# Residual add and RMSNorm on one core: 64 KiB runs, and x and results moved in four groups of every fourth partition

## The chip, the cores and the metric

One NeuronCore of one Trainium2 chip. The metric is device time in microseconds of one execution. The kernel before takes 3724.9 us; its runs lie within 0.1% of each other.

## The reference

```python
x, residual: float32 [32, 2048, 2048]; gamma: ones [2048]; eps = 1e-6
z = x + residual
rms = sqrt(mean(z ** 2, axis=-1, keepdims=True) + eps)
return (z / rms * gamma).astype(float32)
```

65,536 rows of 8 KiB are read twice (x and residual) and written once: 1610.6 MB. There is nothing to reuse.

## The kernel before: what the change touches

The 16 DMA engines take their work from two queues: SyncE's (SP, q1 in the page: x and the stores, 67.2% of the engines' time in the kernel before) and ScalarE's (ACT, q10: the residual, called r below, 32.8%). The packets of a queue that one engine has still to move are called its ring here; the records show the packets, and a ring is called empty when none of them is left. A packet is one record of the trace: the run of one partition, or the 4-byte semaphore packet of 9 ns, here "completion": the records of the kernel before have 3712 for its 232 transfers, 16 each, and as many landings. DVE is VectorE. Tile i of x in four groups is x 0 to x 3, and its stores are store 0 to store 3.

A tile is 128 partitions times 7 rows; each partition's 7 rows are neighbours in memory, one run of 56 KiB. Two slots `z[0]`, `z[1]` take x and are worked on in place; `r_area` of 11 rows takes the residual of two tiles in turn, overlapping by three rows.

```python
R = 7; STEP = 4
z = [sb(f"z{p}", [P, R, D]) for p in range(2)]
r_area = sb("r_area", [P, R + STEP, D])

def sp_turn(sp, t):                       # SyncE, tile i
    i = t.i
    t.wait(sp, "done", -1)                # tile i-1 is finished
    inc(sp.dma_start(out=rows(o_f, i - 1), in_=z[(i - 1) % 2][:, : sizes[i - 1], :]), "s_out", i - 1)
    # ... (last tile cut)
    t.wait(sp, "s_out", -1)               # its store has landed: the slot is free
    load_x(sp, t, 1)                      # x of tile i+1 into that slot

def act_turn(s, t, chain):                # ScalarE, tile i
    for h, (a, b) in enumerate(parts(i)):
        chain.wait()
        t.wait(s, "add_a" if h == 0 else "add_b")
        if h == 0 and i > 0:
            load_r(s, t, 1)               # residual of tile i+1, after the first add of tile i
        inc(act_part(...), "rms_a" if h == 0 else "rms_b", i)   # squares, then the root
```

DVE adds in two parts, takes the reciprocal and scales; ACT squares row by row.

## Time and profile before

| | before |
|---|---|
| time, us (3 runs) | 3724.93 (3724.73 to 3724.96) |
| DVE busy, ACT busy | 62%, 29% |
| DMA share and rate in the middle | 1.00, 434 GB/s |
| bytes at 16 x 27.2 GB/s, an estimate from the packet times of this trace | 3701 us |

The prediction shows the lines that say what bounds it. One more view is needed to follow the argument: the timeline of one tile, cut to what issues transfers (start, length in us, queue, line, what moves).

```profile
1790.20 0.34 SPq L153 DMA_DIRECT2D out_dram<-z  x1
...
1814.55 0.34 ACTq L141 DMA_DIRECT2D r_area<-in_residual_dram  x1
...
1831.02 0.33 SPq L135 DMA_DIRECT2D z<-in_x_dram  x1
...
1841.03 0.34 SPq L153 DMA_DIRECT2D out_dram<-z  x1
```

Read it as two queues that feed the same 16 engines (67.2 + 32.8 = 100.0% of their time). "The hole" below means the moment just before and after 1831.02: a store's last packet is through, the x load that waits for its landing has not begun, and SyncE's ring is empty. The hole is open, and the engine stands idle, when ScalarE's ring is empty too.

### The profile page before, as it was taken

Reading aid. Unit: us, or ns where it says so; the run is one execution under the profiler, and the core shown is the slowest. Engines: PE = TensorE matmul, PEld = TensorE weight load, DVE = VectorE, ACT = ScalarE, POOL = GpSimd, SP = SyncE. Lnnn points to the kernel's source line nnn. Section 1 sums busy time; section 2 is a strip of 40 time slices with the busy share of each in tenths; the row PEclk is TensorE's granted clock in tenths of the full one; section 3 lists DMA queues with packets and bytes.
Section 4 is the critical chain, followed back from the end, with each engine's and each line's share of the span. In section 5 each row is a group of like instructions: output and inputs, shape, how many; then the busy total and the mean of one; then the engine's idle time right before and its main releaser. Section 6 shows DMA issues by size and latency. Waiting matters only on the chain.

```text
span 3723.7 us, 3798 instructions
## 1 busy us (share of the span) xinstructions
DVE 2302.6 (62%) x816; ACT 1072.4 (29%) x1176; POOL 0.2 (0%) x4
## 2 busy tenths in 40 slices
DVE  5666665566665566665566665566665566665566
ACT  2233322233322233322233322233322233322233
POOL 0000000000000000000000000000000000000000
DMA  9999999999999999999999999999999999999999
GB/s 421 431 434 435 434 434 435 434 435 435 434 434 434 434 434 434 434 434 433 434 434 434 434 434 434 434 434 434 434 434 434 434 434 434 434 434 434 434 432 398
DMA packets 32963, 1610.68 MB, mean 433 GB/s; under 512 B 3712, under 2 KB 3776, under 8 KB 3776
## 3 DMA queue, kind: packets, MB, share of 16 engines
q1 hardware_dynamic: 22592, 1082.17, 67.2%
q10 hardware_dynamic: 10368, 528.49, 32.8%
q14 instruction: 3, 0.02, 0.0%
HBM read 1073.77 MB, written 536.87 MB: 433 GB/s over the span
## 4 chain that ended last, share of the span: by engine, by line
DMA 67%; DVE 22%; issue 9%; ACT 2%; SPq 0%; DVEq 0%; ACTq 0%
DMA out_dram<-z 39%; DMA z<-in_x_dram 27%; DVE z L172 15%; DVE z L177 7%; ACT sq_junk L223 1%; ACT rms L231 0%; DVE rstd L197 0%; SPq L259 0%; DVEq L127 0%; DVE r_area L275 0%; ACTq L211 0%; ACTq L127 0%; SPq L141 0%; DVE tail_rstd L292 0%; SPq L162 0%
## 5 line engine op out<-in xcount | busy, mean ns | idle before, releaser
L172 DVE TENSOR_TENSOR z<-z,r_area 128x8192 f32<-128x8192 f32 (+2 forms) x150 | 1109.5, 7437 | 1252.5 <-DMA z<-in_x_dram 1252.5
L223 ACT ACTIVATE sq_junk<-z 128x2048 f32<-128x2048 f32 x512 | 963.4, 1882 | 2617.1 <-DVE z L172 2605.7
L177 DVE SCALAR_TENSOR_TENSOR z<-z,rstd,gamma_tile 128x2048 f32<-128x2048 f32 x505 | 1153.6, 2344 | 5.2
L197 DVE RECIPROCAL rstd<-rms 128x4 f32<-128x4 f32 (+2 forms) x146 | 25.3, 173 | 130.8 <-ACT rms L231 130.8
L223 ACT ACTIVATION_READ_ACCUMULATOR sq_junk<-z 128x1 f32 x512 | 95.5, 186 | 0.0
L231 ACT ACTIVATE rms<-ssq,eps_tile 128x4 f32<-128x4 f32 (+2 forms) x146 | 43.3, 297 | 13.4
L177 DVE SCALAR_TENSOR_TENSOR z<-z,tail_rstd,gamma_tile 128x2048 f32<-128x2048 f32 x7 | 16.2, 2345 | 0.1
L277 DVE LOAD_MASK_SELECT gamma_tile<-r_area x1 | 0.0, 14 | 16.1 <-DMA r_area<-in_gamma_dram 16.1
L277 DVE STREAM_SHUFFLE gamma_tile<-r_area 128x2048 f32<-128x2048 f32 x1 | 2.3, 2290 | 0.0
L275 DVE MEMSET r_area<- 128x2048 f32 x1 | 1.8, 1765 | 0.4 <-issue 0.4
L223 ACT ACT_TABLE_LOAD x1 | 1.3, 1283 | 0.9 <-SPq L77 0.9
L231 ACT ACT_TABLE_LOAD x1 | 1.3, 1283 | 0.1
L231 ACT ACTIVATE tail_rms<-tail_ssq,eps_tile 128x2 f32<-128x2 f32 (+1 forms) x4 | 1.2, 295 | 0.1
L274 DVE MEMSET eps_tile<- 128x1 f32 x1 | 0.1, 59 | 1.0 <-SPq L77 1.0
L292 DVE RECIPROCAL tail_rstd<-tail_rms 128x2 f32<-128x2 f32 (+1 forms) x4 | 0.6, 158 | 0.0
L349 POOL MEMSET const-bfloat16-1.0<- 128x1 bf16 x1 | 0.1, 101 | 0.0
L349 POOL MEMSET const-uint8-127<- 128x1 uint8 x1 | 0.1, 101 | 0.0
L349 POOL MEMSET const-float32-0.0<- 128x1 f32 x1 | 0.1, 98 | 0.2 <-issue 0.2
L349 POOL MEMSET const-float32-1.0<- 128x1 f32 x1 | 0.1, 98 | 0.0
## 6 DMA issues: line engine op xcount, KB each, us to landing
r_area<-in_residual_dram ACTq DMA_DIRECT2D x72, 7168.0 KB, 35.5
z<-in_x_dram SPq DMA_DIRECT2D x71, 7168.0 KB, 27.5
out_dram<-z SPq DMA_DIRECT2D x71, 7168.0 KB, 40.8
z<-in_x_dram SPq DMA_DIRECT2D x3, 2048.0 KB, 17.9
out_dram<-z SPq DMA_DIRECT2D x3, 2048.0 KB, 15.0
r_area<-in_residual_dram SPq DMA_DIRECT2D x1, 5120.0 KB, 25.0
z<-in_x_dram SPq DMA_DIRECT2D x1, 5120.0 KB, 36.7
out_dram<-z SPq DMA_DIRECT2D x1, 5120.0 KB, 26.5
```

The costliest lines, as they stand in the source:

```text
L172: return v.tensor_add(out=s, in0=s, in1=r_area[:, e + a : e + b, :])
L177: ins = v.scalar_tensor_tensor(out=s, in0=s, scalar=rs[:, c + g - a : c + g - a + 1], in1=gamma_tile[:, :], op0=mult, op1=mult,)
L197: v.reciprocal(out=rstd[p][h][:, :n], in_=rms[p][h][:, :n]).then_inc(dve, U)
L223: s.activation(out=sq_junk[:, :], in_=src[:, g, :], func=Act.Square, accum_out=sq[:, g - a : g - a + 1],)
L231: return s.activation(out=rm, in_=sq[:, : b - a], func=Act.Sqrt, bias=eps_tile[:, :], scale=inv_d)
L274: v.memset(eps_tile[:, :], float(eps))
L275: v.memset(stage, 0.0).then_inc(tail_ev["add"], 1)
L277: v.stream_shuffle(gamma_tile[:, :].rearrange("p (a b) -> p a b", a=16), stage, [0] * 32)
L292: v.reciprocal(out=tail_rstd[:, a:b], in_=tail_rms[:, a:b]).then_inc(dve, U)
L349: nc = _bacc.Bacc("TRN2", target_bir_lowering=False, num_devices=1)
```

## The change

Its intent: runs of 64 KiB, so that fewer packets carry the same bytes. Both kernels hold 25 rows a partition: 2 x 7 + 11 before, 2 x 8 + 9 now. So the residual area has only 9 rows, and the residual of the next tile can go out only after seven rows are added. To keep the queue fed all the same, stores and x loads are cut into four groups of 32 partitions (every fourth), and x of a group goes out when the store of that group has landed.

```diff
-    R = 7
-    STEP = 4
+    R = 8
+    AREA = 9
+    Q = 4
...
     def parts(i):
-        return [(STEP, k), (0, STEP)] if i % 2 else [(0, R - STEP), (R - STEP, R)]
+        return [(4, R), (1, 4), (0, 1)] if i % 2 else [(0, 4), (4, R - 1), (R - 1, R)]
...
+    def group(q):
+        return slice(q, P, Q)
+    def load_x(sp, i, q):
+        sp.dma_start(out=z[i % 2][group(q), : sizes[i], :], in_=rows(x_f, i)[group(q)]).then_inc(
+            ev["x_in"][i % 2], U)
...
-    def sp_turn(sp, t):
-        ... (store whole, wait, load whole)
+    def sp_turn(sp, i):
+        def load(q):
+            sp.wait_ge(s_out[q], i * U)
+            load_x(sp, i + 1, q)
+        Turn(i).wait(sp, "done", -1)
+        for q in range(Q - 1):
+            store(sp, i - 1, q)
+        for q in range(Q - 1):
+            load(q)
+        store(sp, i - 1, Q - 1)
+        load(Q - 1)
...
     def act_turn(s, t, chain):
+        t.wait(s, "add_a")
+        squares(s, chain, z[p], a, m, ssq[p][0], 0)      # three rows
+            t.wait(s, "add_b")
+            load_r(s, t, 1)                              # after two adds, 7 rows
+        squares(s, chain, z[p], m, b, ssq[p][0], m - a)
+        ... (root, second half)
```

Cut: names, semaphores, the first tile's residual in a free part of `z[0]`, and the tail (the last tile of 5 rows arrives whole and leaves in three parts; the store of the tile before it leaves in two halves). The order on SyncE: stores 0, 1, 2, then x 0, x 1, x 2, then store 3, then x 3.

More of the change, by code (lines that the diff above doesn't have):

```diff
@@ L38 @@
     n_rows, D = x_f.shape
-    R = 7
-    STEP = 4
+    R = 8
+    AREA = 9
+    Q = 4
     U = 16
-    lead = [3, 5]
-    n_full = (n_rows // P - sum(lead)) // R
-    sizes = lead + [R] * n_full
+    first, final = 3, 5
+    n_full = (n_rows // P - first - final) // R
+    sizes = [first] + [R] * n_full + [final]
     starts = [0]
@@ L50 @@
     last = n_tiles - 1
-    LO = 3
-    n_iter = (last - LO) // 2
+    LO = 1
+    n_iter = (last - 1 - LO) // 2
     HI = LO + 2 * n_iter
-    assert n_iter >= 1
+    assert n_iter >= 1 and last % 2 == 0 and HI == last - 1
     def rows(t, i):
@@ L59, in rows @@
         return t[starts[i] : starts[i] + P * k, :].rearrange("(p r) m -> p r m", r=k)
-    r_full = r_f[starts[2] :, :].rearrange("(n p r) m -> n p r m", p=P, r=R)
+    r_full = r_f[starts[1] : starts[last], :].rearrange("(n p r) m -> n p r m", p=P, r=R)
     inv_d = 1.0 / float(D)
@@ L79 @@
     z = [sb(f"z{p}", [P, R, D]) for p in range(2)]
-    r_area = sb("r_area", [P, R + STEP, D])
+    r_area = sb("r_area", [P, AREA, D])
     eps_tile = sb("eps_tile", [P, 1])
@@ L89 @@
     gamma_tile = ps("gamma_tile", [P, D])
-    names = ["x_in", "r_in", "s_out", "add_a", "add_b", "rms_a", "rms_b", "done"]
+    names = ["x_in", "r_in", "add_a", "add_b", "add_c", "rms_a", "rms_b", "done"]
     ev = {k: [sem(f"{k}{p}") for p in range(2)] for k in names}
-    x_tail = [sem(f"x_tail{k}") for k in range(4)]
+    s_out = [sem(f"s_out{q}") for q in range(Q)]
+    half = sem("half")
     g_in = sem("g_in")
@@ L99, with res, halves @@
     tail_ev = {k: sem(f"tail_{k}") for k in ("add", "rms", "done")}
-    tail = [(0, 2), (2, 4), (4, 6), (6, 7)]
-    def entry(i):
+    tail = [(0, 2), (2, 4), (4, 5)]
+    def res(i, a, b):
         if i == 0:
-            return R + STEP - sizes[0]
-        return 0 if i % 2 else STEP
+            return z[0][:, 5 + a : 5 + b, :]
+        e = 4 if i == last else 0 if i % 2 else 1
+        return r_area[:, e + a : e + b, :]
     def parts(i):
         if i == 0:
-            return [(0, 2), (2, sizes[0])]
-        k = sizes[i] if i < 2 else R
-        return [(STEP, k), (0, STEP)] if i % 2 else [(0, R - STEP), (R - STEP, R)]
+            return [(0, 1), (1, 2), (2, 3)]
+        return [(4, R), (1, 4), (0, 1)] if i % 2 else [(0, 4), (4, R - 1), (R - 1, R)]
+    def halves(i):
+        (a0, b0), (a1, b1), (a2, b2) = parts(i)
+        return [(a0, b0), (min(a1, a2), max(b1, b2))]
     class Turn:
@@ L119, in __init__, with at, whole_x, load_r @@
             self.i, self.it, self.p = i, it, i % 2
-        def at(self, d):
-            n = ((self.i + d) // 2 + 1) * U
-            return n if self.it is None else self.it * (U // 2) + n
+        def at(self, d, u):
+            n = ((self.i + d) // 2 + 1) * u
+            return n if self.it is None else self.it * (u // 2) + n
         def wait(self, eng, kind, d=0):
-            eng.wait_ge(ev[kind][(self.i + d) % 2], self.at(d))
+            u = Q * U if kind == "x_in" else U
+            eng.wait_ge(ev[kind][(self.i + d) % 2], self.at(d, u))
     def inc(ins, kind, i):
         return ins.then_inc(ev[kind][i % 2], U)
-    def load_x(sp, t, d=0):
+    def group(q):
+        return slice(q, P, Q)
+    def load_x(sp, i, q):
+        sp.dma_start(out=z[i % 2][group(q), : sizes[i], :], in_=rows(x_f, i)[group(q)]).then_inc(
+            ev["x_in"][i % 2], U
+        )
+    def whole_x(sp, i):
+        sp.dma_start(out=z[i % 2][:, : sizes[i], :], in_=rows(x_f, i)).then_inc(
+            ev["x_in"][i % 2], Q * U
+        )
+    def load_r(eng, t, d=0):
         i = t.i + d
-        inc(sp.dma_start(out=z[i % 2][:, : sizes[i], :], in_=rows(x_f, i)), "x_in", i)
-    def load_r(sp, t, d=0):
-        i = t.i + d
-        e = entry(i)
-        inc(
-            sp.dma_start(
-                out=r_area[:, e : e + sizes[i], :],
-                in_=rows(r_f, i) if t.it is None else r_full[t.it + (i - 2)],
+        inc(
+            eng.dma_start(
+                out=res(i, 0, sizes[i]),
+                in_=rows(r_f, i) if t.it is None else r_full[t.it + (i - 1)],
             ),
@@ L147, in load_r, with store, store_rows @@
         )
-    def sp_turn(sp, t):
-        i = t.i
-        t.wait(sp, "done", -1)
-        inc(
-            sp.dma_start(out=rows(o_f, i - 1), in_=z[(i - 1) % 2][:, : sizes[i - 1], :]),
-            "s_out",
-            i - 1,
-        )
-        if i == last:
-            return
-        t.wait(sp, "s_out", -1)
-        if i + 1 == last:
-            for k, (a, b) in enumerate(tail):
-                sp.dma_start(
-                    out=z[last % 2][:, a:b, :], in_=rows(x_f, last)[:, a:b, :]
-                ).then_inc(x_tail[k], U)
-        else:
-            load_x(sp, t, 1)
+    def store(sp, i, q):
+        sp.dma_start(out=rows(o_f, i)[group(q)], in_=z[i % 2][group(q), : sizes[i], :]).then_inc(
+            s_out[q], U
+        )
+    def store_rows(sp, i, a, b):
+        sp.dma_start(out=rows(o_f, i)[:, a:b, :], in_=z[i % 2][:, a:b, :]).then_inc(s_tail, U)
+    def sp_turn(sp, i):
[9 more added lines that the diff above has]
+        load(Q - 1)
     def add(v, i, a, b):
-        e = entry(i)
         s = z[i % 2][:, a:b, :]
-        return v.tensor_add(out=s, in0=s, in1=r_area[:, e + a : e + b, :])
+        return v.tensor_add(out=s, in0=s, in1=res(i, a, b))
     def scale(v, i, a, b, rs, c=0):
@@ L190, in dve_turn @@
         t.wait(v, "r_in")
-        (a0, b0), (a1, b1) = parts(i)
-        inc(add(v, i, a0, b0), "add_a", i)
-        inc(add(v, i, a1, b1), "add_b", i)
-        for h, (a, b) in enumerate(parts(i)):
+        for k, (a, b) in zip(("add_a", "add_b", "add_c"), parts(i)):
+            inc(add(v, i, a, b), k, i)
+        for h, (a, b) in enumerate(halves(i)):
             n = b - a
@@ L199, in dve_turn @@
             ins = scale(v, i, a, b, rstd[p][h])
+            if h == 0 and i == last - 1:
+                ins.then_inc(half, 1)
         inc(ins, "done", i)
@@ L215, in next, with squares @@
             self.n += 1
-    def act_part(s, chain, src, a, b, sq, rm):
+    def squares(s, chain, src, a, b, sq, c):
         for g in range(a, b):
-            if g > a:
-                chain.wait()
+            chain.wait()
             chain.next(
@@ L226, in act_part, with root @@
                     func=Act.Square,
-                    accum_out=sq[:, g - a : g - a + 1],
+                    accum_out=sq[:, c + g - a : c + g - a + 1],
                 )
             )
+    def root(s, chain, sq, rm):
         chain.wait()
-        return s.activation(
-            out=rm, in_=sq[:, : b - a], func=Act.Sqrt, bias=eps_tile[:, :], scale=inv_d
-        )
+        return s.activation(out=rm, in_=sq, func=Act.Sqrt, bias=eps_tile[:, :], scale=inv_d)
     def act_turn(s, t, chain):
         i, p = t.i, t.p
-        for h, (a, b) in enumerate(parts(i)):
-            chain.wait()
-            t.wait(s, "add_a" if h == 0 else "add_b")
-            if h == 0 and i > 0:
-                load_r(s, t, 1)
-            inc(
-                act_part(s, chain, z[p], a, b, ssq[p][h], rms[p][h][:, : b - a]),
-                "rms_a" if h == 0 else "rms_b",
-                i,
-            )
-    stage = r_area[:, 5:7, :].rearrange("p r m -> p (r m)")
+        (a, b), (a1, b1), (a2, b2) = parts(i)
+        m = b - 1 if i else b
+        t.wait(s, "add_a")
+        squares(s, chain, z[p], a, m, ssq[p][0], 0)
+        if i == last - 1:
+            load_r(s, t, 1)
+        elif i:
+            t.wait(s, "add_b")
+            load_r(s, t, 1)
+        squares(s, chain, z[p], m, b, ssq[p][0], m - a)
+        n = b - a
+        inc(root(s, chain, ssq[p][0][:, :n], rms[p][0][:, :n]), "rms_a", i)
+        c = min(a1, a2)
+        n = b1 - a1 + b2 - a2
+        if i == 0 or i == last - 1:
+            t.wait(s, "add_b")
+        squares(s, chain, z[p], a1, b1, ssq[p][1], a1 - c)
+        t.wait(s, "add_c")
+        squares(s, chain, z[p], a2, b2, ssq[p][1], a2 - c)
+        inc(root(s, chain, ssq[p][1][:, :n], rms[p][1][:, :n]), "rms_b", i)
+    stage = z[0][:, 3:5, :].rearrange("p r m -> p (r m)")
     stage = stage.rearrange("p (a b) -> p a b", a=16)[:, :, : D // 16]
     def sync_program(sp):
-        load_x(sp, Turn(0))
+        whole_x(sp, 0)
         load_r(sp, Turn(0))
@@ L263, in sync_program @@
         load_r(sp, Turn(1))
-        load_x(sp, Turn(1))
-        for i in range(1, n_tiles):
-            sp_turn(sp, Turn(i))
+        whole_x(sp, 1)
+        for i in range(1, last):
+            sp_turn(sp, i)
+        (a0, b0), (a1, b1) = halves(last - 1)
+        sp.wait_ge(half, 1)
+        store_rows(sp, last - 1, a0, b0)
+        Turn(last).wait(sp, "done", -1)
+        store_rows(sp, last - 1, a1, b1)
         for k, (a, b) in enumerate(tail):
             sp.wait_ge(tail_ev["done"], k + 1)
-            sp.dma_start(
-                out=rows(o_f, last)[:, a:b, :], in_=z[last % 2][:, a:b, :]
-            ).then_inc(s_tail, U)
+            store_rows(sp, last, a, b)
     def vector_program(v):
@@ L286, in vector_program @@
         t = Turn(last)
+        t.wait(v, "x_in")
         t.wait(v, "r_in")
@@ L294, in tail_scale @@
             scale(v, last, a, b, tail_rstd, a).then_inc(tail_ev["done"], 1)
-        for k, (a, b) in enumerate(tail):
-            v.wait_ge(x_tail[k], U)
+        for a, b in tail:
             add(v, last, a, b).then_inc(tail_ev["add"], 1)
-            if k:
-                tail_scale(k - 1)
-        tail_scale(len(tail) - 1)
+        for k in range(len(tail)):
+            tail_scale(k)
     def scalar_program(s):
@@ L317, in scalar_program @@
         for k, (a, b) in enumerate(tail):
-            chain.wait()
             s.wait_ge(tail_ev["add"], k + 2)
-            act_part(
-                s, chain, z[last % 2], a, b, tail_ssq[:, a:b], tail_rms[:, a:b]
-            ).then_inc(tail_ev["rms"], 1)
+            squares(s, chain, z[last % 2], a, b, tail_ssq, a)
+            root(s, chain, tail_ssq[:, a:b], tail_rms[:, a:b]).then_inc(tail_ev["rms"], 1)
     sync_program(nc.sync)
@@ L326 @@
     scalar_program(nc.scalar)
-    nc.gpsimd.wait_ge(ev["s_out"][(last - 1) % 2], ((last - 1) // 2 + 1) * U)
-    nc.gpsimd.wait_ge(s_tail, U * len(tail))
+    for q in range(Q):
+        nc.gpsimd.wait_ge(s_out[q], (last - 1) * U)
+    nc.gpsimd.wait_ge(s_tail, U * (2 + len(tail)))
     ids = [a.num for a in sems]
```

## The prediction

> **What bounds the kernel now.** I read the page first: part 1 (no engine near full), then the DMA lines of parts 2 and 3.
>
> ```profile
> DVE 2302.6 (62%) x816; ACT 1072.4 (29%) x1176; POOL 0.2 (0%) x4
> ...
> DMA  9999999999999999999999999999999999999999
> ...
> DMA packets 32963, 1610.68 MB, mean 433 GB/s; under 512 B 3712, under 2 KB 3776, under 8 KB 3776
> ...
> q1 hardware_dynamic: 22592, 1082.17, 67.2%
> q10 hardware_dynamic: 10368, 528.49, 32.8%
> ```
>
> The reader is to see that the packets of q1 (everything SyncE issues: x and the stores) and of q10 (the residual loads of ScalarE) fill 67.2 + 32.8 = 100.0% of 16 engines' time. Next the windows view over two long stretches, whose last columns are DMA share and GB/s:
>
> ```profile
> 100.00:1600.00 1500.00, 926.82 (x327) 431.77 (x473) 0.00 (x0) 1.00 1.00 434
> 1700.00:3500.00 1800.00, 1114.81 (x389) 517.92 (x568) 0.00 (x0) 1.00 1.00 434
> ```
>
> Share 1.00, all the way. So the chain of waits, which says "DMA out_dram<-z 39%", shows latencies of queued transfers, not empty engines. SyncE's own waits say the same:
>
> ```profile
> SPq L135 <- DMA out_dram<-z: 2828.4, 71, 43.0
> SPq L153 <- DVE z L177: 735.1, 73, 32.2
> ```
>
> x of tile i+1 waits for the store of tile i-1 to land (71 times, 40 us each), yet nothing idles, because the residual load fills that hole. One tile in the chain:
>
> ```profile
> 1790.20 40.80 DMA out_dram<-z
> 1831.02 27.52 DMA z<-in_x_dram
> 1858.63 15.17 DVE z L172 x2
> ```
>
> The store lands at 1831.02, x goes out at once. The timeline has the residual load issued at 1814.55, and the page's part 6 gives it 35.5 us: it flies until 1850, 19 us past the hole.
>
> From the trace's packet records: a run of 56 KiB (7 rows of one partition) takes 2116 ns and one of 8 KiB 309 ns, so (2116 - 309) / 49152 B = 0.03676 ns per byte (27.2 GB/s an engine) and about 8 ns fixed. The next packet starts 3 ns before the end of the last, so a data packet costs some 5 ns beyond its bytes, and a semaphore packet (9 ns) 6 ns. Followed engine by engine, none has gaps of even half a microsecond in sum from 2.0 us (first packet) to some 3717 us. The period of a 7-row tile, (3586.59 - 335.02) / 64 tiles between starts of adds in the chain, is 50.81 us; 24 packets x 2.113 + 3 x 0.006 = 50.73, so all but 0.08 us (a few slow packets) is packets. The kernel is at the floor of its bytes: 1610.68 MB at 16 x 27.2 GB/s is 3701 us, and of the remaining 24 us some 7 are start and end.
>
> [...] So over 2% faster (under 3650 us) would need 441 GB/s; the bytes don't change. [...] No trace of before shows a 32-partition transfer. [...]
>
> **The change part by part.**
>
> *Runs of 64 KiB.* 72 tiles of 7 rows become 63 of 8 (with 3 and 5 as remainder). Data packets per engine: before 77 x-loads, 74 r-loads and 77 stores of 8 = 1824; after x 63 x 8 + 2 x 8 = 520, r 65 x 8 = 520, stores 63 x 8 + 5 x 8 = 544, sum 1584. That is 240 x 5 ns = 1.2 us saved. This is all that longer runs can give.
>
> *Groups.* An x load or store becomes four DMAs, so completions go from 232 (3712 small packets / 16) to about 580 (65 r, 254 x, 257 stores, 4 gamma): 348 x 6 ns = 2.1 us added on each engine. SyncE issues some 9 DMAs of 0.33 us in 58 us: no bound. Engine time in sum: +0.9 us.
>
> *DVE and ACT.* From the groups: adds 2.17 us a row, scales 2.28, squares 2.04. With T the arrival of x and r: adds end at T + 17.4 (a and b, 7 rows, at 15.2), first root at 17.5, scales of four rows to 26.8, second half to T + 36.1. The period at the DMA floor is 24 x (2.116 + 8192 x 0.00003676 = 2.417, less 0.003) + 9 x 0.006 + 0.08 = 58.1 us, which is 50.8 per 7 rows, as now. DVE has 22 us to spare.
>
> *The moved waits: the only place where much can be lost.* The residual area has 9 rows for 8-row slots, so r of the next tile can go out only after seven rows are added (T + 15.2, not T + 6.7), and SyncE holds the fourth store back and x of the fourth group behind that. Hand schedule, E = end of the last x packet on a typical engine, a packet 2.414 us: the semaphore comes 0.5 us after the last packet and the slowest engine some 2.5 us after the typical one (landing records of before spread by 3.6 to 5.8 us), so T = E + 3. r is issued at E + 18.2; [...] its first packet comes 4 to 5 us after the issue (measured in before: 3.9 to 5.6 us), so E + 22.7. SyncE's ring alone does 9.4 packets until then; of 14 (stores 0-2, x 0-2, store 3) 4.6 are left, alternating one for one with r: 4.6 x 2 x 2.414 = 22.2, so store 3 ends at E + 44.9. Its landing on the slowest engine (+3), the semaphore (+0.5) and the first packet (+1.1, the latency of the very first load) leave the ring empty 4.6 us. r then has 8 - 4.6 = 3.4 packets, 8.2 us. Covered, with 3.6 us to spare; before, it was 19 us less the same 5. Next tile's stores are ready (done at T + 36 = E + 39), so no second hole follows.
>
> *Start.* Tile 1 comes whole; x of tile 2 waits for group stores of a small tile with no r in flight: about 1 us idle. *End.* The last tile (5 rows) is no longer split on arrival, its three parts stream out behind the 8-row store; by the same arithmetic the DMA runs almost dry once: about +1 us.
>
> Sum: 3724.9 + 0.9 + 1 + 1 = 3728, holes of steady state nil in the central case.
>
> **Rivals.** (a) *The hole opens.* If the margin of 3.6 us is overdrawn by m, each of some 62 tiles loses m: 1 us gives 3790, 2 us 3850 (slower by 3%). For it: spread between engines' landings grows in before to 12 us on the residual queue late in the run. Against it: [...] r alone during the hole runs at full rate. About one in six for a visible loss, one in fourteen beyond 2%. (b) *Groups of 32 partitions are split badly*[...] One in twenty-five. (c) *It is hidden anyway, and a shade faster*: shorter tail and fewer slow packets, 3720 to 3723. Possible, since only 7 us of head and tail and 16 of packet costs are there to gain at all. (d) *64 KiB does not fit one descriptor* and is cut in two: 1500 more packets x 5 ns = +8 us, still the same.
>
> **Range and chances.** The centre is 3728. The floor (3701 of bytes, 7.6 of data packets, 3.5 of completions, 7 of ends) is 3719, so the low end is 3720; the high end, 3770, allows 0.7 us of hole per tile. [...] Slower by over 2% (3799): (a) 0.07 and (b) 0.04.
>
> **What would show it.** Right: DMA share 1.00 and 434 GB/s in a long window; about 25,300 data packets (1584 x 16) and 9,280 small ones; 64 KiB packets of 2.417 us; period 58.1 us; q1 and q10 still summing to about 100%; DVE waiting on x some 22 us per tile. Wrong by (a): share of 0.96 to 0.99 in every slice, gaps on engines between the fourth store and the fourth x. Wrong by (b): share still 1.00 but GB/s well under 434, packets far longer than 2.4 us. Wrong altogether: if a 64 KiB packet cost less per byte than one of 56.

## The result, and the profile after

| | before | after |
|---|---|---|
| median us (4 runs each) | 3724.88 | 3983.69 (3982.35 to 3986.61) |
| ratio | | 1.0696, 95% interval 1.0677 to 1.0714 |
| profiled run, span us | 3723.7 | 3981.1 |
| period of a tile, per 8 rows, us | 58.1 (50.81 x 8/7) | 62.2 |

Slower by 7%, outside the range. A ratio here is the mean time of one kernel's fast runs over that of the other's in the same rounds, so it is not quite the ratio of the medians quoted.

The page of the kernel after, parts 2 and 3:

```profile
GB/s 421 411 392 420 399 402 410 390 415 396 400 411 400 411 400 408 403 400 412 400 409 402 400 411 400 400 411 400 413 398 411 411 400 411 400 400 410 390 421 379
DMA packets 34694, 1610.73 MB, mean 405 GB/s; under 512 B 9280, under 2 KB 9344, under 8 KB 9344
...
q1 hardware_dynamic: 25616, 1085.34, 65.9%
q10 hardware_dynamic: 9072, 525.34, 30.5%
```

The same bytes, and the packet counts that the prediction named (9280 small ones, 34694 - 9344 = 25350 large), but the two queues now fill 96.4% instead of 100.0%. So about 3.6% of every engine's time stands empty, some 145 us. It is spread over all slices (the GB/s line). The windows view (last columns: DMA share, GB/s) says so too, and says that there is more, because the rate fell by 7% where the share fell by 4%:

```profile
100.00:1600.00 1500.00, 861.19 (x313) 396.15 (x432) 0.00 (x0) 1.00 0.96 404
1700.00:3500.00 1800.00, 1039.67 (x377) 478.72 (x522) 0.00 (x0) 1.00 0.97 405
```

So packets also became longer: those of 64 KiB on SyncE's queue take 2.53 us in the mean, 2.418 in the median. SyncE's own waits: apart from two waits for DVE at the start (33.6 us; before, 73 waits, 735 us) it waits in the loop only for stores to land:

```profile
SPq L149 <- DMA out_dram<-z: 3612.7, 252, 38.2
```

And one tile in the timeline (issues of SyncE and ScalarE):

```profile
1840.24 0.47 SPq L149 DMA_DIRECT2D z<-in_x_dram  x1
1840.75 1.87 SPq L170 DMA_DIRECT2D out_dram<-z  x3
1849.43 17.36 DVE L195 TENSOR_TENSOR z<-z,r_area 128x8192 f32<-128x8192 f32 x3 [25.36 <-DMA z<-in_x_dram]
1854.12 10.13 SPq L149 DMA_DIRECT2D z<-in_x_dram  x3
...
1864.30 0.60 SPq L170 DMA_DIRECT2D out_dram<-z  x1
1864.77 0.34 ACTq L161 DMA_DIRECT2D r_area<-in_residual_dram  x1
...
1902.41 0.47 SPq L149 DMA_DIRECT2D z<-in_x_dram  x1
```

Store 3 goes out at 1864.30, the residual at 1864.77 (tile's arrival + 15.3 us, as predicted), x 3 at 1902.41 when store 3 has landed. What the engines did around that moment is in the trace's packet records. One engine, in the same times; "c" is a completion packet, r a packet of the residual. The records do not name the engine: it was followed by matching each start to the end before it, and across an empty stretch the match is a guess.

```
  start   us     what                 start   us     what
1868.17  2.418   x 1                1889.90          c of x 2
1870.58  2.418   r  (first)         1889.91  2.418   r
1873.00  2.418   x 1                1892.32  2.418   store 3
1875.41  2.418   r                  1894.74  2.418   r
1877.83          c of x 1           1897.15  2.418   store 3
1877.83  2.418   r                  1899.57  2.418   r  (eighth, last)
1880.25  2.418   x 2                1901.98          c of store 3, c of r
1882.66  2.418   r                           1.69    nothing
1885.07  2.418   x 2                1903.68  3.258   x 3
1887.49  2.418   r                  1906.94  3.301   x 3
                                    1910.24  2.418   store 0 of the next tile
```

Three things are to be seen. The last r packet and store 3 end at the same moment, so nothing covers the hole. The two x 3 packets behind it are long. And after a completion packet of SyncE's queue the other queue has its turn: r, c, r, started at 1875.41, 1877.83 and 1877.83.

Over all engines and tiles: each engine stands idle in 62 holes, 2.35 us in the mean (145.6 us); the first packet behind a hole takes 3.136 us in the mean, the second 3.534, every later one 2.42, so (0.72 + 1.12) x 62 = 114 us. Together 260 us, against the 259 that the change costs.

### The profile page after: what moved, and what is told of

It reads as the page before. It is cut to its first block, busy times and chain, and to the rows that moved or that the text cites. A ratio compares the mean times of both kernels' runs of the same rounds, so it can differ in the third digit from the quotient of the medians.

```text
span 3981.1 us, 4005 instructions
## 1 busy us (share of the span) xinstructions
DVE 2300.7 (58%) x842; ACT 1059.7 (27%) x1157; POOL 0.2 (0%) x4
## 2 busy tenths in 40 slices
DMA packets 34694, 1610.73 MB, mean 405 GB/s; under 512 B 9280, under 2 KB 9344, under 8 KB 9344
## 4 chain that ended last, share of the span: by engine, by line
DMA 94%; SPq 3%; DVE 1%; issue 1%; another core or an unknown queue 1%; ACT 0%; ACTq 0%; DVEq 0%
DMA out_dram<-z 93%; SPq L170 2%; SPq L149 1%; DVE z L200 1%; DVE z L195 1%; DMA z<-in_gamma_dram 0%; DMA z<-in_x_dram 0%; ACT sq_junk L246 0%; SPq L292 0%; DVE z L311 0%; ACT rms L256 0%; DVE rstd L219 0%; ACTq L161 0%; DVE tail_rstd L329 0%
## 5 line engine op out<-in xcount | busy, mean ns | idle before, releaser
L219 DVE RECIPROCAL rstd<-rms 128x4 f32<-128x4 f32 (+1 forms) x128 | 22.3, 174 | 58.2 <-ACT rms L256 58.2
L256 ACT ACTIVATE rms<-ssq,eps_tile 128x4 f32<-128x4 f32 (+1 forms) x128 | 38.0, 297 | 11.7
```

Source lines behind the costliest of these rows:

```text
L219: v.reciprocal(out=rstd[p][h][:, :n], in_=rms[p][h][:, :n]).then_inc(dve, U)
L256: return s.activation(out=rm, in_=sq, func=Act.Sqrt, bias=eps_tile[:, :], scale=inv_d)
```

## The experiments

Theory A, after the comparison: the ring of x and stores is empty between store 3 and x 3, r ends just then, and everything lost follows from that hole. Rival B: groups of 32 partitions, or runs of 64 KiB, are slow in themselves. Further rivals for the long packets came up on the way. Twelve kernels ran, all of them correct.

One column carries through: for each run, the idle time of an engine plus what its packets took beyond their bytes at 27.2 GB/s and 8 ns, both worked out from the packets of the kernel before (mean of 16 engines, from the packet records), beside the time above the kernel before in the same rounds.

| run | median us | above before | idle | long packets | sum, less 4.9 of before |
|---|---|---|---|---|---|
| the change | 3983.7 | 258.8 | 146.1 | 119.9 | 261.1 |
| e1_order | 3732.4 | 7.1 | 6.0 | 7.7 | 8.8 |
| e2_late_r | 3986.2 | 260.9 | 142.5 | 124.9 | 262.5 |
| e3_r_groups | 3844.2 | 119.0 | 19.8 | 108.9 | 123.8 |
| e4_whole | 3827.6 | 102.3 | 24.5 | 91.3 | 110.9 |
| e5_later_r | 3877.5 | 152.8 | 40.2 | 118.9 | 154.2 |
| e7_held_stores (1 run) | 4146.2 | 421.4 | 260.6 | 168.1 | 423.8 |
| e8_before_late_r | 4017.1 | 292.3 | 160.0 | 140.7 | 295.8 |
| e9_mid_r | 3905.3 | 180.1 | 70.1 | 117.3 | 182.5 |
| e10_two_groups | 3728.3 | 3.1 | 1.6 | 7.6 | 4.3 |
| e12_one_behind | 3752.5 | 27.5 | 3.5 | 30.2 | 28.8 |

The last column follows the third within a few microseconds in all but e4 (9 off; its profiled run was 4.2 us above its median). It has to, as an engine is either idle or moving a packet: the table says where the time went, not why.

### e1_order: all stores ahead of all loads

```diff
-        for q in range(Q - 1): store(sp, i - 1, q)
-        for q in range(Q - 1): load(q)
-        store(sp, i - 1, Q - 1)
-        load(Q - 1)
+        for q in range(Q): store(sp, i - 1, q)
+        for q in range(Q): load(q)
```

> The changed kernel with one thing altered: all four group stores of a tile are issued before the first x group, and nothing waits behind store 3 but x 3, so SyncE's ring always holds x 0 to x 2 while store 3 lands. Theory A (the +259 us are 62 holes of 2.35 us per engine between store 3 and x 3, plus two slow packets after each hole): holes and slow packets go, 3722 to 3740 us, DMA share 1.00, 434 GB/s. Rival B (groups of 32 partitions or 64 KiB runs are slow in themselves): stays within 1% of the changed kernel, 3945 to 4020 us.

3732.37 us, ratio to before 1.002 (1.0004 to 1.0037). Theory A; B falls: eight-row slots, 64 KiB runs and groups of 32 are all still there. The windows view, from 300 to 3300 us:

```profile
300.00:3300.00 3000.00, 1846.72 (x672) 848.61 (x927) 0.00 (x0) 1.00 1.00 434
```

and SyncE's waits, where the wait for DVE is back (SyncE has issued all of a tile before the next tile is finished):

```profile
SPq L149 <- DMA out_dram<-z: 2361.8, 252, 24.1
SPq L170 <- DVE z L198: 1027.5, 63, 30.2
```

Packets of 64 KiB take 2.421 us in the mean. The 7 us left are the tail: 15 of 16 engines stood 6 us empty before the last tile's first store.

### e2_late_r: the residual later

```diff
         if elif i: t.wait(s, "add_b")
-            load_r(s, t, 1)
...
         squares(s, chain, z[p], a1, a1 + 1, ssq[p][1], a1 - c)
+        if i and i != last - 1: load_r(s, t, 1)
         squares(s, chain, z[p], a1 + 1, b1, ssq[p][1], a1 + 1 - c)
```

> The changed kernel with the residual load of the next tile issued later on ScalarE: after the first square of the second half, about 4.4 us later in each tile. Theory A: r then starts 1.8 packets later and still has about 2 to 3 packets (5 to 7 us) on each engine when store 3 ends, which covers the hole of 2.35 us: 3722 to 3750 us, although a load is issued later. A reader of the chain who takes DVE's wait for data as the cost expects the later load to lengthen the tile: 62 x up to 4.4 us, so 4050 to 4260 us. Rival B: no change, 3945 to 4020 us.

3986.2 us: no change. The theory's number is missed, and the one of "no change" is met. The edit did less than intended. Relative to the issue of x 2 the load moved from 1.0 to 3.0 us, less than one packet and not the 4.4 us expected. It went out when the square before it was dispatched, not when that ended; the timeline of the change has the same in its last tile but one, where a square of 1.88 us and the load that follows it in the program both start at 3913.20. On most engines r now outlasts store 3 by one packet (2.5 us in the mean, in the change 0.0), but the slowest engine's store 3 lands 3.0 us after the mean engine's (in the change 0.55), a packet later as well, and the wait is for the slowest. The run doesn't settle between the two, except that a later residual cost nothing.

### e3_r_groups: four completions for the residual, too

```diff
+            for q in range(Q):
+                eng.dma_start(out=res(i, 0, sizes[i])[group(q)], in_=src[group(q)]).then_inc(ev["r_in"][i % 2], U)
```

> The changed kernel with the residual load split into the same four partition groups, issued at the same place as before. Theory A' (each semaphore packet takes a turn in the alternation of the two queues, so the x and store queue with its 3 to 4 completions loses turns to r, and r runs dry just when store 3 ends): now r loses three turns too, about 3 packets of r (7 us) are left when store 3 ends, the hole is covered: 3722 to 3760 us. If semaphore packets take no turns, the hole stays: 3945 to 4020 us.

3844.2 us, between the two numbers. The part about turns held: idle time fell from 146 to 20 us per engine, and behind store 3's completion most engines had three r packets left (some two; in the change none). The edit does one thing more, it issues the residual over 2.4 us instead of 0.34, so the run alone does not put all of this down to turns; the records show these directly, a completion of r (1876.74 on one engine) between two packets of SyncE's queue. The long packets stayed (109 us). So open holes and long packets are not one thing: where x 3 follows r without a recorded gap, its first packet still takes 2.90 us in the mean (461 such packets), while the first r packet of a tile in the change, which joins an engine that SyncE's queue keeps busy, takes 2.42. Why the one is long and the other is not, the records don't show.

### e4_whole: one group of 128 partitions

```diff
-    Q = 4
+    Q = 1
```

> The changed kernel with one group of 128 partitions (whole stores and x loads, 64 KiB runs kept). Theory A: a tile's store (8 packets, 19.3 us) ends before r's first packet comes (about 22 us after the last x), so each tile has a hole of 2 to 5 us, and the first packets behind it may be slow: 3860 to 4100 us. Rival B1 (the groups are what is slow): about 3728 us. It also tells what the slow packets need: if a whole load after a hole has one or two slow packets, it is the restart that is slow; if none, it takes a group of every fourth partition.

3827.6 us, slower than before by 2.6% (1.0237 to 1.0285), a little below the expected 3860, and faster than the change. Now the engines run dry between the store and the first r packet, because the whole store ends before r comes, as expected. The first r packet behind the store and the last x packet before the next store are long (2.90 and 3.24 us in the mean). It takes no groups to have holes and long packets.

### e5_later_r: the residual after the last square

```diff
         squares(s, chain, z[p], a2, b2, ssq[p][1], a2 - c)
+        if i and i != last - 1: load_r(s, t, 1)
```

> The run with the later residual load had moved it by only 2.0 us (the load goes out when the square before it is dispatched, not when it ends), 0.8 packets. Here it goes out after the last square of the tile, some 8 us later than in the changed kernel, 3.4 packets. Theory A (hole between store 3 and x 3 that r has to cover): r has 3 to 4 packets left when store 3 ends, holes go. If the slow x 3 packets belong to the hole, 3722 to 3770 us; if they stay without holes, as in the run with r in groups, 3830 to 3870 us. If later r lengthens the tile in itself (r on the path), above 4000 us.

3877.5 us, near the second number, but not for the reason given there. Idle time between store 3 and x 3 is gone, other idle time came: r is now so late that SyncE's ring runs dry at the end of store 3 before r's first packet. Idle time 40 us, long packets as before, now the first r packet (3.1 us) and the last r packet before the next store (3.6 us, where they are long). A place of r that is safe on both sides was not found here.

### e6_rotated: another group last

```diff
-        return slice(q, P, Q)
+        return slice((q + 3) % Q, P, Q)
```

> The changed kernel with the four groups in the order 3, 0, 1, 2: the last one stored and loaded is partitions 2, 6, 10 and so on. If the slow x packets belong to a set of partitions [...], they now are in the first x group and the last is clean. If they belong to the place of the last x group in the sequence, nothing changes: 3980 us within 1%, both packets behind the hole at 3.1 and 3.5 us.

4054.1 us in one run, state unknown. The long packets are at the same place, 3.126 and 3.545 us, with another set of partitions: the place matters, not the partitions. The number expected for that, within 1% of 3980, was missed: the time is another 70 us up (idle 185 us, long packets 152 us, some also on other x and r packets). That is not explained and was not followed; with one run of unknown state it may not be the kernel's.

### e7_held_stores: no store issued while x 3 moves

```diff
         Turn(i).wait(sp, "done", -1)
+        Turn(i).wait(sp, "x_in")
```

> The changed kernel in which SyncE waits for the landing of a tile's x before it issues the stores of the tile before. Rival G (the two packets of x 3 are slow because SyncE issues three stores while they move): the second packet of x 3 falls from 3.5 to about 2.4 us. If they are slow for another reason, it stays. In both cases a second hole of 2 to 3 us opens behind x 3 in each tile, so 4080 to 4180 us.

4146.2 us (one run). The second x 3 packet is clean, 2.42 us, as rival G said. But the lost time is not gone: two other packets are long instead, the last store packet before the first x (3.2 us in the mean) and the last r packet before store 3 (3.5 us). In e4_whole a packet is long at the same kind of place while SyncE issues nothing for 15 us and more. So the issuing alone does not explain it. What the change, e4, e5 and e8 show: behind an empty stretch the first load packet took 0.72, 0.48, 0.7 and 0.61 us more than a clean one, and at the next change of direction (loads to stores) the last packet before it took 1.12, 0.82, 1.2 (where it is long) and 1.25 us more. e7 fits in part only: behind its second hole the first packet is a store, and it takes 2.46 us, hardly more than 2.42. Sorted by neighbours, in the kernel after (the cases whose place is certain, of 992 each):

```
packet    after ... before      count    mean us
x         r (hole)   x            845    3.141
x         x          store        849    3.513
x         store      x            838    2.421
store     store      x            851    2.418
```

and in the kernel before, which has no open holes, the last x before a store takes 2.121 us of 2.116 (1034 packets). Why the second part waits for the change of direction no run here tells.

### e8_before_late_r: the old kernel with a hole made on purpose

```diff
-            if h == 0 and i > 0:
-                load_r(s, t, 1)
             inc(act_part(...), ...)
+            if h == 1 and i > 0:
+                load_r(s, t, 1)
```

> The kernel before with only its residual load moved from after the first add to after the last square of the tile (some 14 us later). By the prediction's reading the hole between store and x was filled by r in flight; now r is not there: a hole of about 4 us a tile on every engine, 72 x 4 = 290 us, 3900 to 4060 us, with DMA share below 1.00. If r covers nothing that matters, 3725 to 3760 us. It also shows whether packets of 56 KiB behind a hole are slow: one (restart) or two.

4017.1 us, ratio 1.0787 (1.0769 to 1.0805), as theory A said. Seven rows, whole transfers, no groups, three completions a tile: only the moment of the residual load differs from the kernel before, and the same loss appears. Its page and timeline:

```profile
q1 hardware_dynamic: 22592, 1082.17, 63.4%
q10 hardware_dynamic: 10368, 528.49, 32.7%
```

```profile
1854.13 0.33 SPq L135 DMA_DIRECT2D z<-in_x_dram  x1
...
1869.36 0.34 ACTq L141 DMA_DIRECT2D r_area<-in_residual_dram  x1
...
1878.97 0.35 SPq L153 DMA_DIRECT2D out_dram<-z  x1
```

The two queues fill 96.1% of the engines' time, and x goes out at 1854.13 with no residual in flight (the next at 1869.36). Per tile: 2.08 us empty, the first x packet 2.73 us instead of 2.12, the last r packet before the next store 3.37. That is 0.61 + 1.25 us on top of the hole; times 72 tiles, (2.08 + 0.61 + 1.25) x 72 = 284 of 292 us.

### e9_mid_r: the residual in between

```diff
+            squares(s, chain, z[p], a1, a1 + 2, ssq[p][1], a1 - c)
+            load_r(s, t, 1)
+            squares(s, chain, z[p], a1 + 2, b1, ssq[p][1], a1 + 2 - c)
```

> The changed kernel with the residual load after the second square of the second half, between the two earlier runs (2 us later: still too early, r ends a packet after store 3 on most engines; some 8 us later: too late, the ring of x and stores is empty before r comes). Theory A: r is about 2.5 packets longer in flight than in the changed kernel, x 3 starts while r still moves, so no hole, no slow restart and no slow packet before the next store: 3725 to 3770 us. If no place of r serves, because the tile's arrival shifts with it, 3850 to 3990 us again.

3905.3 us: theory A's number is missed, and the other one, "no place of r serves", is met. Idle time is halved (70 us), the long packets stay. The residual did move: its first packet comes 10.0 us after the issue of x 2 (mean of all engines and some 50 tiles; 8.4 in e2_late_r, 6.4 in the change), and on the mean engine r ends 7.1 us behind store 3 (2.5 and 0.0), which is the 2.5 packets and more that were expected. But the engines draw apart: the slowest engine's store 3 lands 5.8 us behind the mean engine's (3.0 and 0.55), and x 3 waits for the slowest. Why they draw apart was not followed. Sliding r does not give a fine control over the hole.

### e10_two_groups: two groups, stores first, tail row by row

```diff
-    Q = 4
+    Q = 2
-    tail = [(0, 2), (2, 4), (4, 5)]
+    tail = [(k, k + 1) for k in range(5)]     # adds and scales interleaved; order on SyncE as in e1_order
```

> 64 KiB runs with two groups of every second partition, both stores issued ahead of both x loads, and the last tile worked off row by row with adds and scales interleaved. No hole, as in the run with the other order, 254 fewer completions (1.5 us), and the 7 us at the end in which no engine moved anything should shrink to 1: 3720 to 3728 us. If 64 KiB runs save anything it shows here: below 3724; the prediction's count of packets says 1.2 us at most.

3728.30 us against 3725.16, ratio 1.0008 (0.9994 to 1.0022): the same. This is the best form of 64 KiB runs found, and it doesn't beat the kernel before. 5280 small packets instead of 9280, 1.6 us empty at the end.

### e11_blocks: groups of neighbouring partitions

```diff
-        return slice(q, P, Q)
+        return slice(q * (P // Q), (q + 1) * (P // Q))     # on top of e1_order
```

> The run with the other order, but each group is 32 neighbouring partitions. If the engine follows from the partition[...]: packets of 2.4 us but DMA share well under 1.00 and over 4000 us, unless the queue evens it out. If the 32 runs are dealt out two to an engine in order, [...]: packets longer than 2.4 us. If neither matters, 3732 us.

7022 us (one run, state unknown, but the effect is a factor). The page:

```profile
DMA packets 34694, 1610.73 MB, mean 229 GB/s; under 512 B 9280, under 2 KB 9344, under 8 KB 9344
...
q1 hardware_dynamic: 25616, 1085.34, 65.2%
q10 hardware_dynamic: 9072, 525.34, 34.2%
```

Engines full (99.4%), rate halved: x and store packets of 64 KiB take 4.95 us in the middle of their distribution instead of 2.42, and r packets, which did not change, 4.85. Each transfer still has 16 completions (9280 small packets), with two runs before each. So the 32 runs are dealt to all engines in both forms, and the rate is 229 GB/s against 434 in e1_order. Why the packets of neighbouring partitions take twice as long, no run here shows. That the choice of every fourth partition was right, and rival (b) of the prediction wrong, is shown by e1_order beside this.

### e12_one_behind: store 3 one place earlier

```diff
         for q in range(Q - 1): store(sp, i - 1, q)
-        for q in range(Q - 1): load(q)
+        for q in range(Q - 2): load(q)
         store(sp, i - 1, Q - 1)
-        load(Q - 1)
+        for q in range(Q - 2, Q): load(q)
```

> The changed kernel with one swap: store 3 is issued before x 2, not after it, so two packets of x 2 per engine (4.8 us alone) lie in the ring behind store 3 while it lands and x 3 is issued (in the changed kernel the ring stays empty 2.35 us there). If that hole is the whole cause, with the slow packet behind it and the slow one before the next store as its consequences, all go: 3728 to 3745 us, and the timing of the residual load need not be touched. If the last x packets are slow because they are the last before the stores, and not because of the hole, about 1.1 us times 62 tiles stays: 3800 us.

3752.5 us (3740.6 to 3753.5), ratio 1.0064 (1.0047 to 1.0082). One swap takes away 231 of the 259 us, with groups, runs and residual untouched. Two packets behind store 3 cover the hole in most tiles; in some the last packets are still long (30 us in sum), so the number expected was missed by 8 us, and two packets are just short of enough.

## Why the prediction was wrong

Point by point, by its steps.

- **What bounds the kernel: right.** The floor is bytes and packets on 16 engines; e1_order and e10_two_groups come back to it with all the new shapes (434 GB/s, 3732.4 and 3728.3 us).
- **Packets and completions: right.** Counts came out as named, a 64 KiB packet takes 2.418 us (predicted 2.417), and none was cut in two, as rival (d) had it: 24,064 records have 65,536 bytes. The +0.9 us are too small to check: e10_two_groups, with fewer completions, is 3.1 us above before, inside its interval. Longer runs gain nothing because there were only about 9 us of packet costs to gain from. (A slip of no weight: 1584 packets of 5 ns are 7.9 us, not 7.6.)
- **DVE and ACT: right.** Adds end 17.4 us after arrival, r goes out at 15.3.
- **The hand schedule of the moved waits: here it failed.** The step is "of 14 [...] 4.6 are left, alternating one for one with r: 4.6 x 2 x 2.414 = 22.2, so store 3 ends at E + 44.9". On the engine printed above, r's first packet came at E + 21.8 (predicted 22.7; partly luck, as r was issued at E + 16.0, not 18.2, and took 5.8 us to come, not 4.5) and r ended at E + 53.2 (predicted 44.9 + 8.2 = 53.1), but store 3 ended at E + 53.2 as well. Five packets of SyncE's queue were left, not 4.6, and each completion packet took a turn: five packets and two completions (x 1, x 2) alternate with seven r packets, then the eighth r, then store 3's completion. Eight r packets instead of 4.6 go by, and the "3.4 packets, 8.2 us" of cover are nought; three of the 3.4 went to completions, the rest to the fifth packet. The prediction had counted 348 more completions at 6 ns each, but not that each is worth a whole r packet in the alternation. The trace of before already had it: on one engine r at 1823.32, the completion of a store at 1825.43, r again at 1825.44. e3_r_groups supports it from the other side. The rest of the mechanism was foreseen: rival (a) and its sign, gaps between the fourth store and the fourth x at a share of 0.96 to 0.99, are what came.
- **The size of a hole: too large in one term, and one was missing.** The central case had the ring empty 4.6 us, 3 of them for the slowest engine; measured, that engine's store 3 lands 0.55 us behind the mean, and the hole is 2.35 us. Rival (a) said that each of 62 tiles loses m, the idle time, "1 us gives 3790". The holes are 2.35 us, which gives 3871. The other 114 us are long packets behind a hole, which no step of the prediction held and the kernel before, having no open hole, could not show. e8_before_late_r shows them without the change.
- **The chances.** Rival (a) had been given one in six, on a margin of 3.6 us that rested on three estimates of some microseconds each: one and a half packets, in an alternation whose unit is a packet, and three completions were enough to use up all the cover.
- **Start, end:** a few microseconds, as said. e1_order's 6 us at the end, where 1 was expected, go with all five rows being added before the first is scaled: in e10_two_groups, where the last tile arrives whole too but is worked off row by row, 1.6 us are left.

What stays open: why the packets behind a hole are long at all, why the second part falls on the last packet before a change of direction, why the engines draw apart in e2 and e9, and the 70 us more of e6_rotated.

## What to carry to other kernels

Where the DMA engines are the bound, ask of every wait in an issuing program what lies in the rings while it lasts; here a single group load queued behind the store that is waited for was worth 231 us, and issuing all stores ahead of the loads 251. Do not rest on the other queue to cover such a hole unless it is covered by several packets: in these runs the two queues alternate packet by packet, completions count as turns (r, c, r in the records of the change), and finer transfers shift who runs dry first (r in four transfers: 20 us idle instead of 146). And before lengthening runs, divide the packet costs in the trace by their count: what is to be won may be a thousandth.
